# A hybrid decoder step on one core: the memory rows, the scan and the side chains at other places, with other paces and product banks

## The chip, the core and the metric

The kernel runs on one core of a Trainium2 chip. The core has a matrix engine (TensorE, PE in the profile, with a weight load PEld that overlaps it), a vector engine (VectorE, DVE), an activation engine (ScalarE, ACT), GpSimd (POOL) and a queue engine (SyncE, SP) that issues nearly all DMAs here. Each engine works through its own instructions in order and waits at the first one whose inputs or buffers are not there. The metric is the device time of one execution in microseconds, as the median of several runs.

## What is computed

One layer of a decoder in which three branches read the same normalized input. It is computed for 1024 prompt rows and for 8 x 4 sample rows, all in float32.

```python
def memory_kv(mem, mem_norm_g, w_mem_k, w_mem_v):        # 256 memory rows
    m = rmsnorm(mem, mem_norm_g)
    return m @ w_mem_k, m @ w_mem_v

def hybrid_layer(x, conv_state, ssm_state, mem_k, mem_v, ...):
    proj = rmsnorm(x, norm_g) @ w_in                     # 1024 -> 7696 columns
    gm_uv, gm_gate, ssm_z, ssm_xbc, ssm_dt, mem_q, mem_gate = split(proj)
    a_out = gmlp(gm_uv) * silu(gm_gate)                  # 128-row spatial mixing per head
    b_out = mamba2(ssm_z, ssm_xbc, ssm_dt, conv_state, ssm_state)   # conv, chunked scan, gated norm
    c_out = softmax_attention(mem_q, mem_k, mem_v) * silu(mem_gate)
    return x + concat(a_out, b_out, c_out) @ w_out       # 3072 -> 1024

y = rmsnorm(hybrid_layer(x), final_norm_g)               # prompt and sample rows
```

The scan of branch b goes over 8 chunks of 128 rows for each of 2 head groups, 16 chunk steps one behind the other. The sample rows bring their own state and their own memory keys and values (16 MB of them). States, convolution tails, memory keys and values and the gMLP's v rows are outputs too.

## The kernel before

**Precision.** A float32 product is made of three matmuls: each operand is split into a high part H (a copy rounded to fp32r, made on ACT) and a low part L (raw minus H, made on DVE or POOL), and `gemm3` (L330) issues H·H, H·L and L·H for each 128-row slice of the contraction. `split` (L120) makes H and L at once.

**Stages, in order of time.** (1) x rows are normalized, and z and dt columns are made row by row (0 to 125 us); (2) the gMLP's v columns, while the side makes sums of x blocks (to 222 us); (3) 22 *fast units*: each makes 256 output columns for all 1024 rows with seven products instead of eight (`unit`, L493), units 0 to 5 for the convolution, 6 to 9 for q, 10 and 11 for the first half of the memory gate, 12 to 15 for the gMLP gate, 16 to 19 for u, 20 and 21 for the rest of the memory gate (to 833 us); (4) four *plain units* of eight half products for the first third of the output projection, y_a (`unit_plain`, L543, to 988 us); (5) the memory's keys and values in 16 products of 128 rows x 256 columns, each 8 slices (to 1133 us); (6) the second third of the output projection beside the attention (to 1285 us); (7) the last third and the final norm, in 24 products of 128 columns x 384 or 288 rows (to the end). The outputs of a stage go to DRAM and come back when a later stage needs them.

**Product banks.** PSUM has three banks for unit and stage products (`mm_bank`, tags mm0 to mm2), four for everything else (`sd`) and one accumulator. In a fast unit product j writes bank (BANK[j] + 2u) mod 3. `mm()` takes the banks in turn and counts in `mmn`.

**Side chains.** All other work is written as Python generators, a *step* being the code between two `yield`s. After each slice of a product (three matmuls) `gemm3` calls `hook` (L323), which adds the current pace to a counter and, each time that the counter reaches one, puts the next step of the chain that stands first into every engine's program. A fast unit has 28 slices, a plain unit 32. So the pace (steps for each slice) and the yields fix what stands between which matmuls; nothing is decided at run time. A step's PE work stands in PE's own order and stalls the products when its input isn't there.

The chain beside units 6 to 15 (`side_chain`, L1683) does the sample convolution, `conv_out`, the samples' scan (`sample_scan`, state in and out at 0.26 steps a slice), the samples' scores and values (`sample_scores`, `sample_values`, also at 0.26, other steps at 0.8 to 1.0) and the gMLP tables (`gm_prep`). Beside unit 21 `a_load` fetches the a rows, which `a_split` splits into the operands of the plain units, over the buffers of the operands no longer read. Beside the plain units `scan_chain` (L1969) runs: the memory rows (`mem_prep`), the decay rows (`decay_rows`: POOL memsets, eight POOL DMAs into Rt, small row loads), and then `scan` (L1229) with five steps for each chunk, which goes on beside stage 5. `loadB` and `splitB` fetch the scan's results as the operand bH, bL of stage 6 when `SC_.done` says that they are stored.

**Late parts.** `u_split` (L445) puts the H part on ACT and notes the L part in `U.late`; `u_late` (L455) puts the noted L parts on DVE after the second slice of the next product, so that DVE does not wait for ACT ahead of the additions (L502) that free a product's bank.

**The tail.** Before the last stage five y tiles (`y_load`), the x rows of the first row block (`x_reload`) and the final gain (`gfin`) are fetched. Beside block b the c rows of block b + 1 are fetched (`c_load`) and split (`c_split`); `wo_get` splits the weights.

## Time and profile before

| what | us |
|---|---|
| median of 3 runs (lowest, highest) | 1412.37 (1410.91, 1418.32) |
| the profiled execution | 1416.92 |
| its span, first to last instruction | 1415.2 |
| PE busy in it | 1305.3 (92%) |
| DVE busy | 757.8 (54%) |
| ACT busy | 574.7 (41%) |
| POOL busy | 371.0 (26%) |
| mean granted PE clock | 0.958 of full speed |

All rows further down are from the profiled execution; their times are microseconds from its span's start. PE is busy nearly all the time, so a row in which PE is idle, or in which the granted clock is below 1, is time that the kernel loses; all other engines have slack on the average. A row of the timeline shows behind an instruction, in brackets, how long its engine stood idle before it and what ended that.

### The profile page before, as it was taken

Reading aid. Unit: us, or ns where it says so; the run is one execution under the profiler, and the core shown is the slowest. Engines: PE = TensorE matmul, PEld = TensorE weight load, DVE = VectorE, ACT = ScalarE, POOL = GpSimd, SP = SyncE. Lnnn points to the kernel's source line nnn. Section 1 sums busy time; section 2 is a strip of 40 time slices with the busy share of each in tenths; the row PEclk is TensorE's granted clock in tenths of the full one; section 3 lists DMA queues with packets and bytes.
Section 4 is the critical chain, followed back from the end, with each engine's and each line's share of the span. In section 5 each row is a group of like instructions: output and inputs, shape, how many; then the busy total and the mean of one; then the engine's idle time right before and its main releaser. Section 6 shows DMA issues by size and latency. Waiting matters only on the chain. (4 is left out here: it accounts for less than half of the span.)

```text
span 1415.2 us, 22019 instructions
## 1 busy us (share of the span) xinstructions
PE 1305.3 (92%) x8187; PEld 1098.8 (78%) x8187; DVE 757.8 (54%) x1260; ACT 574.7 (41%) x1163; POOL 371.0 (26%) x395
## 2 busy tenths in 40 slices
PE   8999998999889999999999987999777879997996
PEld 7999996787667777666788866767666779997986
DVE  6112536899544554433576653666677446643443
ACT  6222323554322243211477543455656334322232
POOL 4401623222435331221244303333322100000112
PEclk9999999999989999999999999999887899999998
DMA  7232221333345465374555543334555466656442
GB/s 232 71 100 80 81 84 37 103 101 107 98 122 165 139 206 176 117 227 122 160 174 165 209 132 101 118 90 149 177 161 161 141 197 216 194 162 212 147 146 95
DMA packets 215360, 200.76 MB, mean 142 GB/s; under 512 B 28445, under 2 KB 182129, under 8 KB 215253
## 3 DMA queue, kind: packets, MB, share of 16 engines
q1 hardware_dynamic: 214484, 198.95, 45.4%
q8 instruction: 65, 1.06, 0.3%
q0 software_dynamic: 768, 0.40, 0.2%
q14 instruction: 43, 0.34, 0.1%
HBM read 136.61 MB, written 62.43 MB: 141 GB/s over the span
## 5 line engine op out<-in xcount | busy, mean ns | idle before, releaser
L447 ACT ACTIVATE uh<-wst 128x512 fp32r<-128x512 f32 x88 | 55.3, 629 | 131.1 <-PE ps_mm L339 118.2
L455 DVE TENSOR_TENSOR ul<-wr,uh 128x512 fp32r<-128x512 f32 x82 | 70.8, 863 | 43.9 <-ACT uh L447 43.9
L127 DVE TENSOR_TENSOR wl<-wr,wh 128x512 fp32r<-128x512 f32 (+3 forms) x53 | 52.5, 1012 | 60.3 <-ACT wh L124 59.7
L447 ACT ACTIVATE uh<-wr 128x512 fp32r<-128x512 f32 x82 | 51.2, 625 | 77.8 <-PE ps_mm L339 74.8
L2272 POOL TENSOR_TENSOR xres<-xres,gfin 128x1536 f32<-128x1536 f32 (+3 forms) x6 | 14.3, 2385 | 250.7 <-ACT junk L2266 250.7
L455 DVE TENSOR_TENSOR ul<-wst,uh 128x512 fp32r<-128x512 f32 x88 | 66.0, 750 | 21.7 <-ACT uh L447 21.7
L338 PE MATMUL ps_mm<-bH,wh 128*128 128x384 f32 (+1 forms) x192 | 64.8, 337 | 6.8 <-ACT bH L124 5.8
L433 POOL TENSOR_TENSOR wst<-wr 128x512 f32<-128x512 f32 x22 | 28.9, 1314 | 135.1 <-DMA wr<-in_w_in_dram 81.6
L339 PE MATMUL ps_mm<-bL,wh 128*128 128x384 f32 (+1 forms) x192 | 63.1, 329 | 0.1
L340 PE MATMUL ps_mm<-bH,wl 128*128 128x384 f32 (+1 forms) x192 | 63.0, 328 | 0.0
L338 PE MATMUL ps_mm<-xB11H,uh 128*128 128x512 f32 x120 | 50.8, 423 | 7.2 <-DVE go L502 5.1
L996 DVE SCALAR_TENSOR_TENSOR ps_sd<-raw,vecs,ps_sd 128x512 f32<-128x512 f32 x72 | 54.2, 753 | 1.7
L124 ACT ACTIVATE wh<-wr 128x512 fp32r<-128x512 f32 (+3 forms) x60 | 46.9, 812 | 15.2 <-PE ps_mm L340 8.3
L338 PE MATMUL ps_mm<-xB22H,uh 128*128 128x512 f32 x120 | 49.7, 414 | 3.6 <-DVE go L502 3.6
L340 PE MATMUL ps_mm<-xB21H,ul 128*128 128x512 f32 x120 | 47.6, 396 | 2.3 <-DVE ul L455 2.3
L338 PE MATMUL ps_mm<-xB21H,uh 128*128 128x512 f32 x120 | 49.3, 411 | 0.0
L338 PE MATMUL ps_mm<-xT1H,uh 128*128 128x512 f32 x120 | 49.1, 409 | 0.0
L339 PE MATMUL ps_mm<-xB11L,uh 128*128 128x512 f32 x120 | 48.9, 407 | 0.0
L340 PE MATMUL ps_mm<-xB11H,ul 128*128 128x512 f32 x120 | 48.4, 403 | 0.0
L340 PE MATMUL ps_mm<-xB22H,ul 128*128 128x512 f32 x120 | 47.7, 397 | 0.0
L339 PE MATMUL ps_mm<-xB22L,uh 128*128 128x512 f32 x120 | 47.7, 397 | 0.0
L339 PE MATMUL ps_mm<-xB21L,uh 128*128 128x512 f32 x120 | 47.5, 395 | 0.0
(504 smaller groups left out, 4312.9 us busy)
## 6 DMA issues: line engine op xcount, KB each, us to landing
wr<-in_w_in_dram SPq DMA_DIRECT2D x56, 512.0 KB
wr<-in_w_out_dram SPq DMA_DIRECT2D x24, 512.0 KB
kv<-in_cache_mem_k_dram SPq DMA_DIRECT2D x16, 512.0 KB
kv<-in_cache_mem_v_dram SPq DMA_DIRECT2D x16, 512.0 KB
xt<-in_x_prompt_dram SPq DMA_DIRECT2D x8, 512.0 KB
z_d<-gt SPq DMA_DIRECT2D x32, 128.0 KB
v_d<-gt SPq DMA_DIRECT2D x32, 128.0 KB
xc_d<-cd SPq DMA_DIRECT2D x16, 256.0 KB
```

The lines of the kernel that those rows point to most:

```text
L124: ACT.activation(out=H, in_=raw, func=AF.Copy)
L127: leng.tensor_tensor(out=L, in0=raw, in1=rb(H), op=ALU.subtract)
L338: PE.matmul(out=ps, lhsT=lH, rhs=rH, start=(first and k == k0), stop=False)
L339: PE.matmul(out=ps, lhsT=lH, rhs=rL, start=False, stop=False)
L340: PE.matmul(out=ps, lhsT=lL, rhs=rH, start=False, stop=(last and k == k0 + kn - 1))
L433: POOL.tensor_tensor(out=t1, in0=A_(u, 2, 1), in1=A_(u, 2, 2), op=ALU.add)
L447: ACT.activation(out=h, in_=src, func=AF.Copy)
L455: DVE.tensor_tensor(out=l, in0=src, in1=rb(h), op=ALU.subtract)
L996: DVE.scalar_tensor_tensor(out=ps, in0=raw[:, 512 * h + j:512 * h + j + 512], scalar=cw(ct, j), in1=ps, op0=ALU.mult, op1=ALU.add)
L2272: eng.tensor_tensor(out=t[:, 0:nf, c0:c0 + w], in0=t[:, 0:nf, c0:c0 + w], in1=gc.unsqueeze(1).to_broadcast([128, nf, w]), op=ALU.mult)
```

## The change

No matmul is added or removed: PE has 6301 rows of program before and after. The instructions of the other engines are the same too, but for two DMAs that store the memory rows' H and L parts (1 MB each) and two that load them again. What changes is where things stand:

- **Banks.** Fast units use banks one further on; the plain units start at bank 0 (`mmn[0] = 2`).
- **Side steps.** `dt_chain` is cut into more steps (pace 0.25 for 0.3 in units 0 to 5). In units 6 to 15 quick steps go at 1.15 for 0.8 to 1.0, streams at 0.32 for 0.26, and `sample_scan` and `gm_prep` have more yields between steps that depend on each other. `conv_out` comes after the samples' values.
- **Memory rows.** `mem_prep` runs beside units 14 and 15, ahead of `gm_prep`, and stores its result in DRAM (`mem_d`); `mem_load` fetches it in the third plain unit.
- **Decay rows and scan.** `decay_rows` runs ahead of `a_load`, beside unit 20. `scan` begins with the first plain unit, at 0.47 steps a slice for 0.45, and goes on beside stage 5 at 0.28 for 0.37.
- **Splits of a.** Their L parts are made late; both parts of B22 follow product 6 of unit 21.
- **Tail.** Three c rows of block 1, the x rows of block 0 and the final gain are fetched within the attention's last steps; `c_load` runs further ahead and stands before `y_load`; x rows have a tile for each block.

```diff
-            ps = banks[j] = mm_bank((BANK[j] + 2 * u) % 3)
+            ps = banks[j] = mm_bank((BANK[j] + 2 * u + 1) % 3)
...
     def dt_chain(pool):
...
         DVE.scalar_tensor_tensor(out=ab, in0=xr, scalar=-1.0, in1=xr, op0=ALU.mult, op1=ALU.max)
+        yield
...
         ACT.activation(out=a_b, in_=a_b, func=AF.Exp)
+        yield
...
-    set_pace(0.3)
+    set_pace(0.25)
...
         split(psb[:32, 0:256], B3[0:32], B3[32:64], ACT, DVE)
+        yield
+        yield
...
+        for _ in range(2):
+            yield
         DVE.tensor_tensor(out=h3(xde), in0=h3(xdt), in1=hb(te_s, 32, NH), op=ALU.mult)
-        yield
-        yield
+        for _ in range(3):
+            yield
         split(xde, X3[0:32], X3[64:96], ACT, DVE)
+        for _ in range(3):
+            yield
...
-        set_pace(0.26)
+        set_pace(0.32)
...
-        set_pace(1.0)
+        set_pace(1.15)
...
+    mem_d = dpool.tile([2, 128, KD, 256], F32, name="mem_d")
+
+    def mem_prep(p):
+
+        g = p.tile([128, D], F32, name="mg_b")
+        SP.dma_start(out=g, in_=mem_norm_g.to_broadcast([128, D]))
+        HL = [p.tile([128, KD, 256], F32R, name="mem" + e) for e in "HL"]
...
+        for _ in range(5):
+            yield
...
+        for j in range(4):
+            rs[j // 2].s2(j % 2)
+            yield
+        for e in range(2):
+            SP.dma_start(out=mem_d[e], in_=rb(HL[e]))
+        yield
...
-            for _ in range(5):
+            for _ in range(7):
                 yield
...
-            yield
+            for _ in range(4):
+                yield
             ps = sd()
             PE.matmul(out=ps[:32, 0:256], lhsT=rep.rearrange("p b t -> p (b t)"), rhs=w4.rearrange("p h b t -> p (h b t)"),
...
-        with tc.tile_pool(name="cop", bufs=1) as p:
-            yield from conv_out(p)
         with tc.tile_pool(name="samp", bufs=1) as p:
             yield from sample_scan(p)
...
+        with tc.tile_pool(name="cop", bufs=1) as p:
+            yield from conv_out(p)
+        with tc.tile_pool(name="memp2", bufs=1) as p:
+            yield from mem_prep(p)
         yield from gm_prep()
...
-        set_pace(0.8)
+        set_pace(1.15)
...
+    def a_load():
+        yield from decay_rows()
...
-            split(AB.t[nm][:, ks, :], OA[nm][0][:, ks, :], OA[nm][1][:, ks, :], ACT, DVE)
+            src, H, L = AB.t[nm][:, ks, :], OA[nm][0][:, ks, :], OA[nm][1][:, ks, :]
+            ACT.activation(out=H, in_=src, func=AF.Copy)
+            U.late.append((L, src, H))
...
+    def a_last():
+        a_split("B22", 0)()
+        a_split("B22", 1)()
...
     def scan_chain():
-        yield from mem_prep()
-        m2_ctx.close()
-        yield from decay_rows()
         SC_.p = c_ctx.enter_context(tc.tile_pool(name="ssd", bufs=1))
...
-        set_pace(0.45)
-
+        set_pace(0.47)
+
+    def mem_load():
+        for e, t in enumerate((M.H, M.L)):
+            SP.dma_start(out=rb(t), in_=mem_d[e])
+
+    mmn[0] = 2
     for i in range(4):
-        spill(2 * i, y_d, AF.Copy, {0: scan_open} if i == 0 else None, X=OA, xs=AB.s)
+        spill(2 * i, y_d, AF.Copy, {0: {0: scan_open}, 2: {0: mem_load}}.get(i), X=OA, xs=AB.s)
...
-    set_pace(0.37)
+    set_pace(0.28)
...
             c_split(0, k, 2)
-            yield
+            if k < 6:
+                c_load(1, k // 2, 1)
+            yield
+        xres[0] = hp.tile([128, 3, D], F32, name="xres0")
+        x_rows(0)
+        gf.append(hp.tile([128, D], F32, name="gfin"))
+        SP.dma_start(out=gf[0], in_=final_norm_g.unsqueeze(0).to_broadcast([128, D]))
+        yield
...
         for ct in range(8):
+            if b < 2 and ct < 5:
+                c_load(b + 1, ct + 3, 1)
+            elif b < 1:
+                c_load(2, ct - 5, 1)
             y_load(8 * b + ct + 5)
-            if b < 2 and ct < 6:
-                if ct == 0:
-                    c_load(b + 1, 0, 1)
-                c_load(b + 1, ct + 1, 1 if ct < 5 else 2)
```

Three places show what this does to the order on an engine.

SP beside unit 15, before the change, where the gMLP tables are fetched (gg_d is the spilled gate, wr a weight tile, wsp the spatial weights that PE transposes first):

```order
L189 DMA gg_d<-go 128x512
L189 DMA gg_d<-sr 128x2x32
L214 DMA wr<-in_w_in_dram 128x4x256
L1613 DMA os_d<-os_s 128x8x32
L1635 DMA wsp<-in_gm_w_spatial_dram 128x8x128
L1636 DMA gnb_b<-in_gm_norm_b_dram 128x1024
L1637 DMA gng_b<-in_gm_norm_g_dram 32x1024
```

And after it:

```order
L189 DMA gg_d<-go 128x512
L189 DMA gg_d<-sr 128x2x32
L214 DMA wr<-in_w_in_dram 128x4x256
L1665 DMA mem_d<-memH 128x2048
L1665 DMA mem_d<-memL 128x2048
L1687 DMA wsp<-in_gm_w_spatial_dram 128x8x128
L1688 DMA gnb_b<-in_gm_norm_b_dram 128x1024
```

The two stores of the memory rows, 1 MB each, now stand directly ahead of wsp.

PE within the first plain unit (22), before, in the second half of its products (L316 are the transposes of the normalized memory rows):

```order
L338 MATMUL ps_mm<-xB11H,uh 128x512
L339 MATMUL ps_mm<-xB11L,uh 128x512
L340 MATMUL ps_mm<-xB11H,ul 128x512
L316 MATMUL ps_sd<-ident,xn 128x128 x4
L338 MATMUL ps_mm<-xB11H,uh 128x512
L339 MATMUL ps_mm<-xB11L,uh 128x512
L340 MATMUL ps_mm<-xB11H,ul 128x512
```

And after, in its fourth product (L1162, L1163, L1166 and L1200 are the first PE work of the scan's chunk 0, lines 1155, 1156, 1159 and 1193 of before):

```order
L338 MATMUL ps_mm<-xB22H,uh 128x512
L339 MATMUL ps_mm<-xB22L,uh 128x512
L340 MATMUL ps_mm<-xB22H,ul 128x512
L1162 MATMUL ps_sd<-bc 128x128
L1163 MATMUL ps_sd<-ident,bc 128x128
L1166 MATMUL ps_sd<-ident,xk 128x128 x4
L1200 MATMUL ps_sd<-Rt,Lt 128x512
L338 MATMUL ps_mm<-xB22H,uh 128x512
```

The memory rows' transposes are gone from the unit, and the scan's first matmul stands 25 slices (75 product matmuls) earlier than before, where it came in unit 23.

SP from the end of the attention into the tail, before (gt and y_d belong to stage 6, cr are c rows, ys y tiles, xres x rows):

```order
L1910 DMA y_d<-gt 128x288
L1898 DMA gt<-y_d 128x384
L214 DMA wr<-in_w_out_dram 128x8x128
L1910 DMA y_d<-gt 128x384
L1898 DMA gt<-y_d 128x288
L1910 DMA y_d<-gt 128x384
L1910 DMA y_d<-gt 128x288
L2199 DMA ys<-y_d 128x384 x5
L2206 DMA xres<-in_x_prompt_dram 128x1024 x3
L2213 DMA gfin<-in_final_norm_g_dram 128x1024
L2199 DMA ys<-y_d 128x384
L2173 DMA cr<-c_d 128x384 x2
```

And after:

```order
L2225 DMA cr<-c_d 128x384 x3
L1973 DMA y_d<-gt 128x288
L1961 DMA gt<-y_d 128x384
L2217 DMA xres_12572<-in_x_prompt_dram 128x1024 x3
L2209 DMA gfin<-in_final_norm_g_dram 128x1024
L214 DMA wr<-in_w_out_dram 128x8x128
L1973 DMA y_d<-gt 128x384
L1961 DMA gt<-y_d 128x288
L1973 DMA y_d<-gt 128x384
L1973 DMA y_d<-gt 128x288
L2250 DMA ys<-y_d 128x384 x5
L2225 DMA cr<-c_d 128x384
```

The first c rows, the x rows and the gain have moved from behind the five ys loads to ahead of the last gt loads.

## Rows read from the trace of the kernel before

**Rows 1.** The page's first part, PE: busy us (share), instructions.

```profile
PE 1305.3 (92%) x8187; PEld 1098.8 (78%) x8187; DVE 757.8 (54%) x1260; ACT 574.7 (41%) x1163; POOL 371.0 (26%) x395
```

**Rows 2.** Busy time by stretch: window and length, then engines, granted PE clock, DMA share, GB/s.

```profile
222.00:245.00 23.00, 19.22 (x86) 14.13 (x87) 13.87 (x35) 9.73 (x19) 5.86 (x8) 0.85 0.10 31
366.00:510.00 144.00, 133.83 (x686) 98.80 (x685) 72.90 (x108) 44.27 (x82) 66.21 (x59) 0.92 0.46 135
510.00:660.00 150.00, 150.00 (x870) 101.56 (x868) 58.83 (x94) 40.58 (x70) 25.11 (x20) 1.00 0.54 175
660.00:700.00 40.00, 36.00 (x164) 27.67 (x163) 18.17 (x29) 10.34 (x16) 8.21 (x9) 0.91 0.53 150
820.00:840.00 20.00, 13.79 (x53) 10.66 (x52) 10.94 (x14) 8.83 (x12) 0.00 (x0) 0.91 0.44 150
840.00:890.00 50.00, 42.74 (x239) 32.81 (x239) 17.02 (x30) 19.10 (x35) 16.29 (x29) 0.93 0.40 115
890.00:988.00 98.00, 91.26 (x606) 68.11 (x605) 61.92 (x106) 51.95 (x120) 35.20 (x42) 1.00 0.36 109
988.00:1133.00 145.00, 112.98 (x854) 97.49 (x852) 94.35 (x152) 82.55 (x191) 36.33 (x45) 0.85 0.55 162
1133.00:1160.00 27.00, 19.32 (x106) 18.48 (x107) 11.67 (x20) 8.93 (x16) 0.00 (x0) 0.87 0.84 245
1290.00:1381.00 91.00, 76.91 (x440) 74.47 (x439) 36.72 (x59) 23.73 (x55) 12.28 (x6) 0.94 0.50 160
```

**Rows 3.** PE's waits, longest in total: total us, times, longest us.

```profile
PE ps_mm L338 <- DVE go L502: 9.8, 3, 5.1
...
PE ps_sd L1155 <- DMA bc<-bc_d: 6.5, 1, 6.5
PE ps_mm L338 <- ACT woH L124: 6.3, 1, 6.3
PE ps_mm L338 <- ACT bH L124: 5.8, 1, 5.8
PE ps_sd L1047 <- POOL csT L1027: 5.1, 1, 5.1
```

**Rows 4.** Timeline of PE in unit 6: start, us, instruction, before and behind the L1047 wait.

```profile
374.00 0.39 PE L339 MATMUL ps_mm<-xT4L,uh 128*128 128x512 f32 x1
...
374.68 0.39 PE L339 MATMUL ps_mm<-xT4L,uh 128*128 128x512 f32 x1
...
382.12 0.63 PE L340 MATMUL ps_mm<-xT4H,ul 128*128 128x512 f32 x1
382.55 0.63 PE L338 MATMUL ps_mm<-xB11H,uh 128*128 128x512 f32 x1
```

**Rows 5.** Timeline of PE, the waits at the start of unit 0.

```profile
222.48 0.50 PE L338 MATMUL ps_mm<-xB11H,uh 128*128 128x512 f32 x1 [2.01 <-DVE gt L384]
...
234.91 0.50 PE L340 MATMUL ps_mm<-xB21H,ul 128*128 128x512 f32 x1 [2.26 <-DVE ul L455]
```

**Rows 6.** Timeline of POOL, first and last instruction of the samples' convolution (nine in all).

```profile
370.90 1.35 POOL L1019 TENSOR_TENSOR cvs<-rs,vecs 128x384 f32<-128x384 f32 x1
...
379.89 0.47 POOL L1027 COPY csT<-rs 128x288 f32<-128x288 f32 x1
```

**Rows 7.** Timelines of SP and of PE, the spatial weights' load and its first reader.

```profile
665.45 0.37 SPq L1635 DMA_DIRECT2D wsp<-in_gm_w_spatial_dram  x1
...
669.54 1.09 PE L1649 MATMUL ps_sd<-ident,wsp 128*128 128x128 f32 x4 [2.34 <-DMA wsp<-in_gm_w_spatial_dram]
```

**Rows 8.** SP's own waits, the one of the scan's first load.

```profile
SPq L1115 <- DMA Rt<-Rraw: 8.6, 4, 6.7
```

**Rows 9.** Timelines of SP and ACT at the tail's start.

```profile
1292.75 1.38 SPq L2206 DMA_DIRECT2D xres<-in_x_prompt_dram  x3
...
1296.10 1.28 SPq L2173 DMA_DIRECT2D cr<-c_d  x2
...
1304.11 0.52 ACT L124 ACTIVATE cH<-cr 128x384 fp32r<-128x384 f32 x1 [18.39 <-DMA cr<-c_d]
```

131 lines of the change are left out of this document (68 added, 63 removed).

## Prediction

> **What bounds the kernel now.** The page comes first: PE is busy for 1305.3 of 1415.2 us and every other engine for at most 54% [rows 1]. The change neither adds nor removes a matmul, so its time can only come from what PE loses. PE loses in two ways: it stands idle, or it runs at the lower granted clock. The second view is the table by stretch [rows 2]: length less PE busy is the idle time, and length times (1 - granted clock) is about what the lower of the two levels (1.2 for 2.4 GHz) cost there. Six stretches in ten carry it, and one by far the most:
>
> - 222 to 245 (start of unit 0): 3.8 idle + 3.5 clock = 7.2
> - 366 to 510 (side chain's start, samples' scan): 10.2 + 11.5 = 21.7
> - 510 to 660 (sample streams): 0
> - 660 to 700 (gMLP tables): 4.0 + 3.6 = 7.6
> - 820 to 840 (last fast unit to first plain one): 6.2 + 1.8 = 8.0
> - 840 to 890 (scan's start): 7.3 + 3.5 = 10.8
> - 890 to 988 (plain units beside the scan): 6.7 + 0 = 6.7
> - 988 to 1133 (keys and values beside the scan): 32.0 + 21.8 = 53.8
> - 1133 to 1160 (stage 6 begins): 7.7 + 3.5 = 11.2
> - 1290 to 1381 (tail): 14.1 + 5.5 = 19.6
>
> Together 146.6 us, the most that the change could touch. Third come the waits and their timelines [rows 3 to 9], which say what each loss is. What the clock does is seen in the product matmuls: 0.23 us apart before PE's wait for L1047, and 0.43 apart after it [rows 4]. So a wait of several microseconds is paid nearly twice, and one that goes takes its slow stretch along.
>
> One slice of a unit is three matmuls, so 0.69 us [rows 4]; a keys-and-values slice has half the columns, which I estimate at 0.35.
>
> **The change part by part.** Gains are counted against the profiled execution (1416.9, span 1415.2).
>
> *Banks and dt_chain, 7.2 now.* Unit 0 waits 2.0 us because its bank is the one that the last v product still holds, then 2.3 because DVE, stuck behind dt_chain's chain of ACT results, makes ul late [rows 5]. With the bank one further on, unit 0 finds one that was freed two products earlier; dt_chain's steps stand four slices apart, 2.8 us, against instructions below 1 us. I take a gain of 5 (3 to 7).
>
> *Side chain's start, 21.7 now.* PE waits 5.1 for the samples' convolution [rows 3], which takes POOL 370.9 to 380.4 [rows 6]. Its first PE reader now comes 12 slices behind the chain's start, 8.3 us and two sample matmul groups, against 9.5: a wait of 0 to 1. The next loss is an addition (L502) that stands on DVE behind a split waiting for ACT, one of three such waits of 9.8 together [rows 3]; now two to three yields lie between such steps. The slow stretch behind both should go in part, but sixteen 8-column matmuls for the decay stay where they are and may hold the clock down. Gain 14.5 (6 to 20).
>
> *Streams at 0.32 for 0.26, 0 now.* A 512 KB load every 3.1 slices for 3.8. The stretch moves 175 GB/s at a DMA share of 0.54 [rows 2]; 1.2 times that is 0.65. Below zero there is nothing to gain, since PE is never idle there. Cost 1 (0 to 6).
>
> *Memory rows beside units 14 and 15, 7.6 now.* Their PE work is moved, not added, and hides where the products are. New are the waits. From the loads to the first transposes lie 11 slices, 7.6 us, and a sample group: about right for 1.5 MB at the tail's rate (below), a square on ACT and a product on DVE, so 0 to 3 of wait. Then two 1 MB stores go out on SP directly ahead of wsp. From the last memory transposes to wsp's first reader lie 27 matmuls, 6.2 us. SP can issue the stores only after the last split, by my estimate 2 us later, and wsp 1.4 after that; wsp needs 4.1 from issue to use when nothing large is ahead [rows 7]: ready at 7.7, a wait of 1.5. If the 2 MB go first, at the 280 GB/s of the tail (2.6 MB between 1292.8 and 1304.1, less an estimated 2 for the latency, [rows 9]), it is 7 us more: a wait of 7 to 8. The tail's c rows, which landed only 8 us after their issue with 2 MB ahead of them [rows 9], are nearest to that case. I take 5.5, and 5 for the clock behind it and 1.5 for the first transposes: 12, a loss of 5 (12 lost to 5 gained). SP's stores of the gate stand behind it, and nobody waits for them. The Trainium skill, "DMA: Bandwidth & Descriptors" (Queues, rings and completion order), says that each DMA engine takes its descriptors in ring order, which speaks against this part: by that, the wait is the 7 to 8 us and the whole sum 2 us worse; by wsp's own row alone it is 1.5 and the sum 4 us better.
>
> *Late splits of a, bank 0 first, 8.0 now.* The two L502 waits here are 6.2 idle: DVE makes a large L part of a ahead of the addition that frees a bank, and the first plain unit starts in the bank of the last product. Both go. The decay rows now keep POOL beside unit 20, longer than the 6.7 us that SP waits for them now [rows 8], in front of the sums for unit 21; those have about 8 slices (5.5 us) of slack, so 0 to 2 lost. Gain 6 (3 to 8).
>
> *Scan's start, 10.8 now.* PE waits 6.5 for the first bc tile [rows 3]. The cause is on SP: it holds the scan's first load (L1115) for 6.7 us until the Rt DMAs have read a buffer that it lies over [rows 8]. With the decay rows 50 slices earlier that wait is gone; next late is the load itself, issued 8 slices (5.5 us) and a sample group ahead. Gain 7 (3 to 10).
>
> *Scan beside plain units and keys and values, 60.5 now.* The program gives 5 steps to a chunk. Before, 8.8 chunk loops fall into the keys and values, 13.5 slices each; after, 5.9, with 17.9 slices each. In the plain units 10 instead of 7, at 10.6 slices for 11.1. So a step is covered by 0.93 us of products in the keys and values now, 1.53 in the plain units, and the losses for a loop are 6.1 and 1.0. After, the cover is 1.23 and 1.47: on the line between the two rows, 3.6 and 1.5. DVE would then be busy about 80% of a loop (94.4 us in 145 now, a third less time for each loop's work at most [rows 2]), so I take 4.5 rather than 3.6. That makes 5.9 x 4.5 + 10 x 1.5 = 41.6: a gain of 18 (0, if the keys and values keep 6.1 and the plain units rise to 2.5; 38, if they come down to 2). The 2 MB reload in the third plain unit delays an xk load by up to 7 us, with a loop of 14 us ahead: nothing.
>
> *Stage 6 begins, 11.2 now.* PE waits 5.8 for the last split of bH [rows 3], because the scan's last store comes 8 slices before the end. Now it comes 18 before, 3.5 us earlier. Gain 7 (2 to 10).
>
> *Tail, 19.6 now.* ACT stands idle for 18.4 us until the first c rows land, with the x rows and gain ahead of them [rows 9], and the weights' split behind it costs PE 6.3 [rows 3]. That goes, and with it most of what follows in the stretch. But the 2 MB now stand ahead of the last gt loads and the ys loads, whose sums stand on DVE ahead of a weight split: up to 7 us of new wait, of which I take 5, plus 4 for the clock. Gain 9 (0 to 17).
>
> Sum: 5 + 14.5 - 1 - 5 + 6 + 7 + 18 + 7 + 9 = 60.5, so 1416.9 becomes 1356. The profiled execution lies 4.5 above the median of the three runs, 1412.4; the same gain from that gives **1352**.
>
> **The rivals.** *Half of it.* The scan's chain, not its cover, sets the loop (gain 6), the stores are ahead of wsp in full (12 lost) and the tail only trades waits (2 gained): 38.5 of the others + 6 - 12 + 2 = 34.5, 1378. For it: DVE at 80%, one xk buffer, four sd banks. Against it: the same loop ran at 14 us with hardly a wait in the plain units.
>
> *More.* The keys and values come down to the plain units' level, wsp comes in time for what it costs now, the tail is smooth: 38.5 + 36 + 0 + 15 = 89.5, 1323.
>
> *Slower.* One mechanism could do it: the scan begun with the output projection meets in all its 16 loops what it meets in the keys and values now (waits for sd banks that DVE and ACT free late), and more. The other terms give 42.5, so the scan's loss would have to grow from 60.5 to 103, 6.4 for each loop, against 6.1 now at the worst place. At 8 it is 1437. For it: plain units too must split weights on DVE. Against it: 1.0 for each loop there now.
>
> *The scan does not really start earlier,* since its first loads are held again, by the buffers of a: 7 and some 4 of the scan's gain are lost, 1363, within the forecast's reach.
>
> **How the numbers follow.** Forecast, 1336 to 1367: 0.57 (with the last rival). Half: 0.24. More: 0.12. Within 0.5% (7 us, about what a measurement of this kernel can tell from no change): 0.03. Slower: 0.04. The likeliest is 1352. The range runs to both neighbours, 1324 to 1386: it leaves out about half of "more" and the ends of "half", and the slower cases. Faster by over 0.5%: 0.93, the first three; same 0.03; slower 0.04.
>
> **What would show it.** Right, if PE's wait list has lost L1047, bc, woH and bH and the L502 waits; if the keys and values take about 100 us instead of 145, at a clock above 0.9; if a new wait of some 5 us stands at wsp, and a smaller one at the tail's first weight split. Wrong, if the chunk loop stays at 16.5 us there (145 / 8.8) whatever the pace, or if PE waits in the sample streams or for the memory rows.

## The result, and the profile after

The changed kernel takes **1392.38 us** (median of 4 runs, 1390.72 to 1397.39), against 1411.71 for the kernel before beside it: a ratio of 0.9859, 95% interval 0.982 to 0.9898. Forecast were 1352, 1324 to 1386. The direction was right; of a gain of 60.5 us, 19.3 came (26.2 between the two spans, 1415.2 and 1389.0). PE is still the only engine near its limit; the page's first part, as [rows 1]:

```profile
PE 1294.5 (93%) x8187; PEld 1092.4 (79%) x8187; DVE 766.2 (55%) x1262; ACT 575.4 (41%) x1166; POOL 373.6 (27%) x395
```

The table by stretch, with the columns of [rows 2], in stretches of after that hold the same work:

```profile
221.00:244.00 23.00, 22.93 (x111) 17.66 (x110) 18.30 (x34) 12.19 (x20) 7.12 (x12) 1.00 0.20 59
360.00:510.00 150.00, 144.17 (x788) 106.57 (x790) 81.24 (x119) 50.00 (x91) 71.28 (x61) 0.97 0.54 164
510.00:640.00 130.00, 128.09 (x748) 85.71 (x744) 48.22 (x79) 31.87 (x56) 19.96 (x15) 1.00 0.50 161
640.00:700.00 60.00, 49.11 (x213) 37.27 (x204) 28.70 (x40) 18.07 (x30) 13.58 (x15) 0.80 0.51 161
805.00:832.00 27.00, 22.43 (x108) 16.83 (x108) 16.53 (x21) 12.39 (x21) 3.62 (x3) 1.00 0.83 278
832.00:870.00 38.00, 31.69 (x176) 24.41 (x174) 19.24 (x31) 17.34 (x32) 7.76 (x9) 0.96 0.39 121
870.00:1000.00 130.00, 119.57 (x805) 89.51 (x806) 80.29 (x140) 71.32 (x164) 45.25 (x54) 0.98 0.42 127
1000.00:1114.00 114.00, 90.46 (x697) 80.26 (x696) 77.48 (x121) 67.20 (x151) 22.77 (x28) 0.84 0.62 181
1118.00:1142.00 24.00, 19.31 (x113) 19.03 (x112) 7.58 (x14) 5.66 (x10) 0.00 (x0) 0.86 0.85 242
1272.00:1365.00 93.00, 85.27 (x518) 83.77 (x517) 43.13 (x77) 25.54 (x63) 14.00 (x8) 0.94 0.48 151
```

With the prediction's measure (length less PE busy, plus length times one less the clock) each term of its sum has its answer:

| term | lost before | lost after | gain | forecast |
|---|---|---|---|---|
| banks, dt_chain | 7.2 | 0.1, and 1.2 at 252.9 | 5.9 | 5 (3 to 7) |
| side chain's start | 21.7 | 10.3 | 11.4 | 14.5 (6 to 20) |
| streams | 0 | 1.9 | -1.9 | -1 (-6 to 0) |
| memory rows, tables | 7.6 | 22.9 | **-15.3** | -5 (-12 to 5) |
| late splits of a | 8.0 | 4.6 | 3.4 | 6 (3 to 8) |
| scan's start | 10.8 | 7.8 | 3.0 | 7 (3 to 10) |
| scan beside plain units, keys and values | 60.5 | 13.0 + 41.8 | **5.7** | 18 (0 to 38) |
| stage 6 begins | 11.2 | 8.1 | 3.1 | 7 (2 to 10) |
| tail | 19.6 | 13.3 | 6.3 | 9 (0 to 17) |
| sum | 146.6 | 125.0 | 21.6 | 60.5 |

The sum lacks 4.6 us of the spans' difference. Over the whole spans the same measure gives 169.3 us lost before and 145.9 after, 23.4 apart, so some 2 us were won outside these stretches; the 3 that remain it does not see, and no run shows what they are. Of the missing 39 us, the scan's loop has 12, the memory rows 10, and five other places 2.6 to 4 each. PE's list of waits (total us, times, longest), as [rows 3] for before, has new names where most of the old ones stood.

```profile
PE ps_sd L1189 <- DVE BL L127: 7.5, 6, 2.8
PE ps_mm L338 <- DVE gt L1972: 6.5, 2, 4.7
PE ps_sd L1701 <- issue: 6.1, 1, 6.1
PE ps_mm L340 <- DVE wl L127: 5.5, 1, 5.5
PE ps_sd L316 <- issue: 4.8, 1, 4.8
...
PE ps_sd L1162 <- DMA bc<-bc_d: 4.7, 1, 4.7
...
PE ps_mm L340 <- DVE ul L455: 3.8, 1, 3.8
...
PE ps_mm L338 <- DVE go L502: 2.7, 2, 1.5
```

L1701 reads the spatial weights wsp, L316 the memory rows' norm, L1162 opens a chunk of the scan, L1189 is its state product. L1047, woH and bH have left the list, as the prediction asked; bc has not, and the L502 waits have shrunk from 9.8 us to 2.7.

### The profile page after: what moved, and what is told of

It reads as the page before. It is cut to its first block, busy times and chain, and to the rows that moved or that the text cites. A ratio compares the mean times of both kernels' runs of the same rounds, so it can differ in the third digit from the quotient of the medians.

```text
span 1389.0 us, 22033 instructions
## 1 busy us (share of the span) xinstructions
PE 1294.5 (93%) x8187; PEld 1092.4 (79%) x8187; DVE 766.2 (55%) x1262; ACT 575.4 (41%) x1166; POOL 373.6 (27%) x395
## 4 chain that ended last, share of the span: by engine, by line
PE 74%; DVE 6%; DMA 6%; issue 5%; ACT 4%; POOL 2%; SPq 1%; POOLq 0%; ACTq 0%; DVEq 0%
PE ps_mm L338 19%; PE ps_mm L340 18%; PE ps_mm L339 18%; PE ps_sd L1264 1%; PE ps_acc L1617 1%; PE ps_acc L1555 1%; PE ps_sd L1818 1%; PE ps_acc L488 1%; PE ps_sd L1570 1%; PE ps_sd L316 1%; ACT wh L124 1%; DMA gt<-y_d 1%; DMA aB<-a_d 1%; PE ps_sd L488 1%; DVE wl L127 1%
## 5 line engine op out<-in xcount | busy, mean ns | idle before, releaser
L340 PE MATMUL ps_mm<-xT1H,ul 128*128 128x512 f32 x120 | 47.5, 396 | 3.8 <-DVE ul L455 3.8
L339 PE MATMUL ps_mm<-xT1L,uh 128*128 128x512 f32 x120 | 47.4, 395 | 0.0
```

Source lines behind the costliest of these rows:

```text
L339: PE.matmul(out=ps, lhsT=lH, rhs=rL, start=False, stop=False)
L340: PE.matmul(out=ps, lhsT=lL, rhs=rH, start=False, stop=(last and k == k0 + kn - 1))
```

## Experiments

All are edits of the kernel after, and their times stand beside its 1392.4 and its ratio of 0.9859 to the kernel before.

### The scan's loop: both sides alone

```diff
-    set_pace(0.28)
+    set_pace(0.0)
     for blk in range(8):
```

> Change to the kernel after: the scan stands still through the keys and values (pace 0) and its last 5 to 6 loops run behind them with no products beside them. It measures both by themselves. Theory (the loop is a chain through ACT, DVE and POOL that is longer than PE's own 6 us): a loop alone takes 11 us or more, so that even a loop with 12 us of PE's work in the keys and values has no slack where the chain's parts fall together, and the keys and values alone take 50 to 60 us (128 slices, 45 us, and some waits for weights). Rival (a loop alone takes 8 us or less, and the keys and values alone 70 us or more, as their own splits and loads set their time): then the keys and values are the limit and not the scan. In all slower than after: 1400 to 1425.

Measured: 1410.2 (one run). The two stretches, keys and values alone and then four loops of the scan alone (columns as above):

```profile
1003.00:1061.00 58.00, 53.16 (x400) 52.26 (x399) 30.19 (x45) 30.36 (x59) 0.00 (x0) 0.90 0.85 248
1071.00:1118.00 47.00, 28.12 (x196) 19.79 (x196) 32.04 (x54) 23.95 (x58) 16.26 (x19) 0.72 0.24 70
```

A loop alone takes **11.7 us** (11.2 to 12.2, from one state product to the next), with PE busy for 60% of it at a granted clock of 0.72; the keys and values alone take 58 (first to last of their products). Both are what the theory asked for. The first and the last state product, four loops apart:

```profile
1071.55 0.80 PE L1189 MATMUL ps_sd<-xdH,BH 128*128 128x512 f32 x1 [2.44 <-ACT sz L1112]
...
1118.23 0.79 PE L1189 MATMUL ps_sd<-xdH,BH 128*128 128x512 f32 x1 [4.76 <-ACT xdH L124]
```

Together they took 113 in after, with 5.9 loops, and 140 before, with 8.8: (113 - 58) / 5.9 = 9.3 for a loop, and (140 - 58) / 8.8 = 9.3 as well, if the 58 of this one run hold for before too. So a loop costs about the same there at either pace (e6 below, with some 6.5 loops, gives 10.5), and saves no more than 2.4 of its 11.7 us. By the prediction's measure the keys and values alone already lose 4.8 idle and 5.8 to the clock, 10.6 in all, while they move 248 GB/s (181 in after). As far as this stays when the scan stands beside them, it belongs to no loop, and the loops lose (53.8 - 10.6) / 8.8 = 4.9 us each before and (41.8 - 10.6) / 5.9 = 5.3 after; the prediction divided the whole loss by the loops. Beside the plain units a loop takes 14.2 with 10.6 slices of 0.69 in it, so it costs 6.9. A loop moved from the one place to the other is worth 2.4 us, and 2.9 were moved: 7, against the 5.7 measured.

### The scan's loop: pace

```diff
-        set_pace(0.47)          # plain units
+        set_pace(0.60)          # e6: 0.45
...
-    set_pace(0.28)              # keys and values
+    set_pace(0.20)              # e6: 0.37
```

> Change to the kernel after: the scan's pace only, 0.60 steps a slice beside the plain units instead of 0.47, and 0.20 in the keys and values instead of 0.28, so that some 12.5 loops fall into the plain units (8.3 slices each) and 3.6 into the keys and values (25 slices each). Theory (products beside a step decide, as in the prediction's line from 1.0 lost at 1.53 us a step to 6.1 at 0.93): a step has 1.15 us of products in the plain units and 1.75 in the keys and values, so the plain units lose about 4 a loop and the keys and values less than 1: in all some 50 us as in after's 55, the keys and values' loops nearly free of loss. Rival (the splits that keys and values and scan share on ACT and DVE decide there, whatever the pace): the loss for a loop stays at 6 to 8 us in the keys and values, the plain units stay below 2 a loop, and the whole comes to 13 x 1.5 + 3.6 x 7 = 45, 1380 to 1386.

> Change to the kernel after: the scan's pace as in the kernel before, 0.45 and 0.37, with the rest of after kept, so that a loop in the keys and values has 13.5 slices as before and the scan ends some 30 slices earlier. Theory (products beside a step decide): the loss for a loop there rises against after's, as after's was to fall against before's; the stage becomes longer, 1394 to 1402. Rival (the shared splits decide): a loop loses 5.5 to 7 us as in both kernels, the stage has as many loops as in after or half a loop more, and the time is within 4 us of after, 1388 to 1396.

Measured: 1406.5 (ratio 0.9925, 0.9897 to 0.9952) and 1391.6 (0.9829, 0.9776 to 0.9883). Loops from one state product to the next, in the keys and values:

| kernel | slices a loop | mean loop there | stage | loop in plain units | median |
|---|---|---|---|---|---|
| before | 13.5 | 16.1 | 139.9 | 14.6 | 1411.7 |
| e6, pace as before | 13.5 | 16.1 | 126.5 | 14.5 | 1391.6 |
| after | 17.9 | 18.4 | 113.1 | 14.2 | 1392.4 |
| e5, 0.60 and 0.20 | 25 | 17.7 (one) | 88.9 | 13.9 | 1406.5 |
| e7, bL on POOL | 17.9 | 17.4 | 110.4 | 14.3 | 1388.8 |
| e16, bH and bL on POOL | 17.9 | 16.9 | 110.7 | 14.6 | 1390.5 |
| e1, rows earlier | 17.9 | 18.4 | 115.4 | 14.5 | 1394.1 |
| e9, keys' own bank | 17.9 | 19.0 | 112.0 | 14.1 | 1390.4 |
| e12, split earlier | 17.9 | 17.0 | 108.1 | 13.9 | 1383.8 |
| e10, both | 17.9 | 17.4 | 105.4 | 13.8 | 1380.8 |

(The table counts from state product to state product, the expectations from chunk to chunk.) A third more products beside each step make the loop longer, not its loss smaller; the pace of after won nothing over that of before. At 0.60 a loop beside the plain units costs 8.2 instead of 6.9. And e5 shows a second cost, which both theories missed: once the scan has ended, ACT stands for the scan's rows (yb), with the weights' split behind them, and PE behind that. ACT, then PE, of e5:

```profile
1103.55 0.63 ACT L124 ACTIVATE bH<-yb 128x512 fp32r<-128x512 f32 x1 [6.47 <-DMA yb<-yb_d]
...
1105.90 2.11 ACT L124 ACTIVATE wh<-wr 128x512 fp32r<-128x512 f32 x3
```

```profile
1106.60 0.58 PE L338 MATMUL ps_mm<-wh,memH 128*128 128x256 f32 x1 [4.24 <-ACT wh L124]
```

### The scan's loop: amount of work

```diff
-            split(t[:, :, :tsz(c)], bH[:, ks, ts_], bL[:, ks, ts_], ACT, DVE)
+            split(t[:, :, :tsz(c)], bH[:, ks, ts_], bL[:, ks, ts_], POOL, POOL)   # e7: ACT, POOL
```

> Change to the kernel after: the L parts of the scan's rows (bL, 18 subtractions of 0.65 us) are made on POOL, not on DVE. Theory (shared splits on ACT and DVE decide in the keys and values): DVE there is busy for 77 of 114 us and waits for ACT nearly all of the rest, so 11.5 us less of its work shortens the stage by 5 to 11 us: 1381 to 1388. Rival (too few products beside a step): no change but for POOL's slower instructions, 1390 to 1395. A third (POOL, at about 1.3 us for each, becomes late with xdL and MT and holds up DVE by its own accesses): slower, 1395 to 1405.

> Change to the kernel after: both parts of the scan's rows (bH and bL, 36 instructions, about 10 us of ACT and 11 of DVE) are made on POOL, which is busy for 23 of 114 us there; the keys and values then share that much less of ACT and DVE with the scan. Theory (the amount of work that the two share sets the loop): the loops beside the keys and values fall from 20.1, 18.2 and 19.4 to 16 or less, and the stage by 10 us or more: 1376 to 1384, but for what POOL's last parts cost at the start of stage 6. Rival (the order in each queue sets it, as the earlier split showed): loops of 17.5 us or more, 1386 to 1394, or slower where POOL's xdL now stands behind these parts.

Measured: 1388.8 (0.9821, 0.9776 to 0.9865) and 1390.5 (0.9833, 0.9808 to 0.9858). In e16 the stage has 57.8 and 69.8 us of ACT and DVE where after has 67.2 and 77.5, and PE loses as much:

```profile
1002.00:1112.00 110.00, 86.38 (x688) 77.43 (x686) 69.81 (x102) 57.81 (x133) 56.85 (x61) 0.83 0.61 181
```

The loops became 1 to 1.5 us shorter, half of what the theory asked or less, and the medians are 2 to 4 us lower, which their intervals do not tell from none. That the amount of work is a part of it is read from the loops of these traces, and no more. POOL's help was not free either: the weights' splits of 128x512 on DVE took 1058 ns on the average in e16, against 747 in after.

### The scan's loop: order and banks

ACT of after in one loop there: it waits 2.8 us for DVE's gate product, and the next chunk's weighted rows (xdH), the finished rows (sz, which free a bank of sd) and BH stand behind that wait; then PE, which waits for the bank.

```profile
1031.46 0.63 ACT L1097 ACTIVATE sz<-xsD 128x512 f32<-128x512 f32 x1 [2.84 <-DVE xsD L1095]
...
1032.09 0.61 ACT L124 ACTIVATE xdH<-xde 128x512 fp32r<-128x512 f32 x1
1032.61 1.12 ACT L1112 ACTIVATE sz<-ps_sd,vecs 128x128 f32<-128x128 f32 x4
1033.61 0.29 ACT L124 ACTIVATE BH<-ps_sd 128x128 fp32r<-128x128 f32 x1
```

```profile
1033.79 0.69 PE L2051 MATMUL ps_sd<-ident,kst 128*128 128x128 f32 x2 [2.46 <-ACT sz L1112]
```

```diff
 # e1: the finished rows ahead of the norm, into a buffer of their own
+                    yo = SC_.p.tile([128, 512], F32, tag="t1", name="yo", bufs=1)
+                    fy = y_T2(r, 128, gp_, cp_ * 128, yo)
...
 # e9: the keys' transposes
-        ps = sd()
+        ps = acc_bank()
...
 # e12: two steps earlier; e10: e9 and e12
-            if nx:
-                sXsplit(i + 1)
             fs = []
...
+            if nx:
+                sXsplit(i + 1)
             pd = sd()
```

> Change to the kernel after: the scan's scaled output rows of the chunk before (four ACT instructions, y_T2) go into a buffer of their own and are issued before the gate norm of this chunk, no longer behind its square. Theory (crossed queues): in the keys and values ACT stands 2.8 us in every loop for DVE's gate product, and the rows, which free the sd bank that PE asks for next, stand behind it; PE's waits for these rows (13.3 us of idle, and the slow clock behind them) go, the loop falls from about 18.5 to 16.5 us, and the run comes out 8 to 16 us below the kernel after, at 1376 to 1384. Rival (too few products beside each step): the wait only changes its name, 1389 to 1395. Rival (DVE's amount of work): DVE has nothing less to do, 1389 to 1395.

> Change to the kernel after: the transposes of the keys (k_T, one bank of sd for each key product, up to eight of them while the scan runs) use the bank that the units' samples used, which is free here, and no longer one of the four sd banks that the scan takes in turn. Theory (bank ring): with one k_T between, the scan's decay product meets the bank of the rows just transposed (PE waits for ACT's sz L1112) and its state product the bank whose B part DVE is still making (PE waits for DVE's BL); in the plain units, where the scan has the four banks alone, the same loop loses about 1. The waits L1200 and L2051 for ACT's sz (8.5 us) and L1189 for DVE's BL (7.5) go while keys are made, the loops there fall from 20.1, 18.2 and 19.4 to some 16, and the run comes out 6 to 14 us lower, 1378 to 1386. Rival (chain through ACT and DVE, as the two runs before showed that a wait only changes its name): the loops keep 18 us or more, 1389 to 1395.

> As the run with the keys' own bank, and the split of the next chunk's weighted rows (xdH on ACT, xdL on POOL) stands two steps earlier in the loop, ahead of the gate norm for which ACT waits 2.8 us, instead of behind it. Theory (crossed queues, second part): the state product's waits for xdH and xdL (4.6 us and about 1 us in most loops, plain units too) go as well, 4 to 10 us below the run with the bank alone, 1370 to 1380. Rival (the norm's chain itself is what is late): no more than 2 us below that run.

> Change to the kernel after: only the earlier split of the next chunk's weighted rows (xdH, xdL two steps earlier, ahead of the gate norm); the keys' transposes keep their sd bank. Theory (the split behind the norm is the cause, the bank is not): as the run with both, 1379 to 1384, loops of some 16 us in the keys and values. Rival (both are needed, each hides the other): 1387 to 1393, loops of 18 us, PE waiting for ACT's sz (L1112) and DVE's BL as in after.

Measured: e1 1394.1 (0.9838, 0.9803 to 0.9873), e9 1390.4 (0.9837, 0.9808 to 0.9865), e10 **1380.8** (0.9761, 0.9739 to 0.9783), e12 **1383.8** (0.9746, 0.970 to 0.9793). e1's theory fell: PE's waits for sz went, and waits for BL of up to 5.2 us came, where 2.8 had been the longest. e9's fell too, its loops grew. e12's theory held in the time (1379 to 1384), while its loops came to 17.0, not 16. The split alone does nearly all, in the plain units as well (13.8 to 13.9 a loop); whether the bank adds to it is not settled (3 us by the medians, nothing by the ratios). The stretches of e10, plain units and keys and values, against 870 to 1114 above:

```profile
866.00:998.00 132.00, 121.95 (x833) 93.31 (x832) 90.74 (x146) 73.81 (x168) 48.54 (x57) 0.99 0.43 130
998.00:1103.00 105.00, 83.58 (x691) 75.10 (x690) 77.86 (x120) 67.07 (x151) 24.21 (x28) 0.92 0.67 194
```

So 11.4 + 29.8 = 41 are lost there, against 55 in after. The 30 that are left in the keys and values (10.6 of them lost there even without the scan, e17) were not taken away by any run; e15 below, which put more of DVE's order right, changed nothing.

### Memory rows and the spatial weights

In after, SP issues wsp's load 6 us behind the second store of the memory rows, and POOL, whose fills go into the same place, says what for (SP, POOL, PE):

```profile
652.86 0.33 SPq L1665 DMA_DIRECT2D mem_d<-memH  x1
653.58 0.33 SPq L1665 DMA_DIRECT2D mem_d<-memL  x1
659.51 0.38 SPq L1687 DMA_DIRECT2D wsp<-in_gm_w_spatial_dram  x1
```

```profile
659.57 0.20 POOL L1692 MEMSET one_r<- 1x128 f32 x1 [11.13 <-DMA mem_d<-memL]
```

```profile
646.18 1.09 PE L316 MATMUL ps_sd<-ident,xn 128*128 128x128 f32 x4 [4.79 <-issue]
...
663.78 1.08 PE L1701 MATMUL ps_sd<-ident,wsp 128*128 128x128 f32 x4 [6.10 <-issue]
```

```diff
+        with tc.tile_pool(name="wspp", bufs=1, side="right") as wp_:
+            wsp = wp_.tile([128, 8, 128], F32, name="wsp")
             with tc.tile_pool(name="memp2", bufs=1) as p:
                 yield from mem_prep(p)
+            yield from gm_prep(wsp)
```

> Change to the kernel after: the spatial weights wsp get 4 KB of their own, so that their load does not write where the memory rows' parts lie; the stores of the memory rows still stand ahead of it on SP. Theory (buffer): in the trace of after wsp's load was not issued until both stores had landed (issue at 659.5, stores at 652.9 and 653.6), so it will now be issued within 1 us of them and PE's wait of 6.1 us at the first wsp transposes becomes 0 to 2.5, with some slow clock gone: 1382 to 1388. Rival (queue order, as the prediction had it): the load is issued early but its data come only behind the 2 MB of stores; the wait stays 5 us or more, 1390 to 1395.

Measured: 1391.1 (0.9822, 0.9752 to 0.9891). The load was issued at once, and was not early (SP, PE of e2):

```profile
654.12 1.24 SPq L1686 DMA_DIRECT2D wsp<-in_gm_w_spatial_dram  x1
```

```profile
662.40 1.09 PE L1700 MATMUL ps_sd<-ident,wsp 128*128 128x128 f32 x4 [4.58 <-DMA wsp<-in_gm_w_spatial_dram]
```

8.3 us from issue to use, against 4.1 in [rows 7] with nothing ahead, and 4.3 in after, where the buffer had held the load until the stores were done. The theory was wrong and the rival nearly right (a wait of 4.6 where it asked for 5 or more): the stores cost the wait by either road, and the buffer only 1.5 us on top. The Trainium skill, "DMA: Bandwidth & Descriptors" (Queues, rings and completion order), has each engine take its descriptors in ring order; e2 agrees, with 8.3 us behind 2 MB.

Then the rows' own wait was given time (e8, part b), and last the order was changed (e14, below):

```diff
 # (a) conv_samples
+        for _ in range(9):
+            yield
         ACT.activation(out=cvs, in_=cvs, func=AF.Silu)
...
 # (b) mem_prep
-        for _ in range(5):
+        for _ in range(12):
             yield
...
 # (c) attention
-        x_rows(0)
+        for j in range(3):
+            SP.dma_start(out=xres[0][:, j], in_=xp_rows[j * 128:(j + 1) * 128, :])
+            yield
+            yield
```

> Three changes to the kernel after, in stretches that lie far apart and are read one by one in the trace. (a) Side chain's start: nine more steps before ACT's silu of the samples' convolution, and DVE's first instruction that needs POOL's fills two steps later. Theory (ACT and DVE stand for POOL, and the weights' parts behind them are what PE misses): PE's 3.8 us for ul goes, with 3 us of slow clock. Rival (the chain is only as late as before at its next reader): PE waits 3 us or more at the next place. (b) Memory rows: seven more steps between their loads and the norm, one more before and two more behind each product of the norm, two fewer at the end. Theory (10.8 us from load to first transposes against 6 of cover): the 4.8 us wait falls below 1; wsp's wait of 6.1 stays at 5 to 7. (c) The tail: the x rows of the first block are loaded one at a time, two steps apart, and the gain after them. Theory (the last gt load lands 7.6 us after its issue, behind 2 MB): the waits of 1.8 and 5.5 fall to 2 or less together, as does the slow stretch behind them. Rival: the last gt load is still behind a row of x or the gain and 4 us or more stay. All three by theory: some 20 us, 1370 to 1376; by the rivals 1386 to 1392.

Measured: 1383.8 (0.9794, 0.9739 to 0.9849), between its theory and its rivals; by its parts:

(a) The wait for ul went, and one of 3.5 us came at 393 (for an addition that stands on DVE behind the split of the samples' rows); the low clock of that stretch was gone in e8, and two thirds back in e11. That ACT and DVE had stood for POOL is plain in after's rows (ACT, DVE, PE):

```profile
373.15 0.52 ACT L1033 ACTIVATE cvs<-cvs 128x384 f32<-128x384 f32 x1 [5.87 <-POOL cvs L1031]
```

```profile
375.56 0.25 DVE L1342 TENSOR_SCALAR Ls<-accTs 16x32 f32<-16x32 f32 x1 [7.81 <-POOL Cm L1357]
```

```profile
376.46 0.51 PE L340 MATMUL ps_mm<-xT1H,ul 128*128 128x512 f32 x1 [3.78 <-DVE ul L455]
```

(b) The rows' wait of 4.8 went to 0, but wsp's grew from 6.1 to 7.9: the side chain has no slices left there. Unit 15 ends, the rest is drained, and wsp's eight transposes stand in a row with no product between them.

(c) The wait of 1.8 went; of the 5.5, 5.0 stayed. Behind the last gt load stood a second cause, in SP and DVE of e8: the first ys loads are issued only when the last product of stage 6 has read the operand that their buffers lie over, and the weights' split stands on DVE behind their sum.

```profile
1270.09 2.23 SPq L2254 DMA_DIRECT2D ys<-y_d  x5
```

```profile
1272.66 0.55 DVE L2370 TENSOR_TENSOR ys<-ys,ps_mm 128x384 f32<-128x384 f32 x1 [6.87 <-DMA ys<-y_d]
1273.14 1.22 DVE L127 TENSOR_TENSOR wl<-wr,wh 128x1024 fp32r<-128x1024 f32 x1
```

### The scan's start, and stage 6

```diff
 # e3, in scan()
+            if i == 0:
+                for _ in range(3):
+                    yield
             if nx:
                 sA(i + 1)
```

> Change to the kernel after: three more steps between the scan's first chunk and its second (nothing else). Theory (the wait moved to the second chunk): the wait of 4.7 us at the scan's start is that of the second chunk's rows, which can only be loaded when the first chunk's have left their one buffer, 5.5 us ahead of their use; with three steps (6.4 slices, 4.4 us) more, it falls under 1 us and takes about 2 us of slow clock along, while the scan ends three steps later in the keys and values (about 2 us): 1386 to 1390. Rival (the transfers themselves are late whenever they are asked for, as 280 GB/s are moved there): 3 us or more of the wait stay, 1391 to 1397.

Measured: 1386.5 (0.978, 0.9742 to 0.9818). The wait for bc is gone and the stretch runs at full clock, as the theory had it. It had been the wait for the second chunk's load: in after SP issued it at 845.75, when the first chunk had left the one buffer, PE was there 1.4 us later, and the load took 6.1:

```profile
851.87 0.77 PE L1162 MATMUL ps_sd<-bc 128*128 128x128 f32 x2 [4.74 <-DMA bc<-bc_d]
```

In return the scan ends later, and the wait at stage 6's start is again one for bH, 6.7 us.

```diff
 # e4
         y_open(0)
+        y_open(1)
+        vr_load()               # was ahead of outproj
```

> Change to the kernel after: at the start of stage 6 the first two loads of partial sums (gt) are issued ahead of the reload of the memory values (vr), not behind it. Theory (next in the queue): the 4.7 us that PE waits for DVE's first sum there come from SP, which holds the vr load for 4.7 us until its data have been stored, with the gt loads behind; the wait goes, and the slow stretch of 7 us behind it: 1384 to 1388. Rival (the values' parts, vL, become the next late thing, or the gt loads wait for their buffers): PE waits as long somewhere in the next 15 us, 1390 to 1394.

Measured: 1391.6 (0.9816, 0.9777 to 0.9856). In after SP spends 4.65 us on vr, whose rows must first be stored, and gt's loads stand behind (SP, DVE):

```profile
1120.96 4.65 SPq L2092 DMA_DIRECT2D vr<-mv_d  x2
1125.66 0.90 SPq L1961 DMA_DIRECT2D gt<-y_d  x2
```

```profile
1129.56 0.55 DVE L1972 TENSOR_TENSOR gt<-gt,ps_mm 128x384 f32<-128x384 f32 x1 [7.68 <-DMA gt<-y_d]
```

The rival was right: 1.7 of the 4.7 stayed, and 3.4 came at the first attention product, which reads the queries, loaded behind vr.

### The sums

e11: e8, e3 and e4, ys in a buffer that lies free, and 13 steps more ahead of wsp's reader. e13: e10, e3 (pace 0.50), e4, e8 (c) and ys. e14: e13 and e8 (a), the streams at 0.36, and

```diff
-        with tc.tile_pool(name="memp2", bufs=1) as p:
-            yield from mem_prep(p)
         yield from gm_prep()
+        with tc.tile_pool(name="memp2", bufs=1) as p:
+            yield from mem_prep(p)      # row by row, ten steps from load to norm
```

e15: e14, e1 and DVE's hL ahead of the sums.

> All the changes to after that touch other places than the scan's loop, together: side chain's start, memory rows and the tail's x rows as in their run; thirteen steps more between the spatial weights' load and their first reader (wsp landed 8.3 us after its issue when the 2 MB of stores were ahead of it and no buffer held it, and was held 5.5 us more by the buffer); the tail's first partial sums (ys) in a buffer that does not lie over the operand of the product before (their load was issued only when that product had ended); the scan's second chunk three steps later; the first gt loads ahead of vr. Theory: each place loses what its wait was: wsp 7.9 to under 1.5, the tail's 5.0 to under 2, the scan's start 4.7 to under 1, stage 6 to 4 or so (the operand's last split is next, since the scan ends later), side start 3.5 stays; with the clock behind them some 30 us less than after, 1358 to 1368. Rival (each wait has another a microsecond behind it, as at the samples' start): half of it, 1372 to 1380.

> The mended places together, with the memory rows and the side chain's start as in after: keys' own bank, earlier split of the weighted rows, three steps before the scan's second chunk with its pace at 0.50 for 0.47, gt ahead of vr, x rows of the tail one at a time, ys in a buffer of its own. Theory (the terms stand side by side): from after's 1392.4 less 11.5 (scan's loop), 6 (scan's start), 6.5 (tail) and 0 to 2 (stage 6), 1366 to 1370. Rival (what is won beside the keys and values is waited for in stage 6): 1372 to 1380.

> As the run before, and in the side chain: the gMLP tables are made first and the memory rows after them, row by row, with ten steps from the loads to the norm; nine more steps before ACT's silu at the chain's start; the three streams at 0.36 for 0.32, which makes room for both. Theory (the memory rows cost after 13 us more than the tables alone had cost before, as they were given neither time nor a place behind the tables): the loss of 20 us in that stretch falls to 7 (as before, 7.6) and the samples' start by some 4: 1349 to 1356. Rival (the loss follows the memory rows: their stores now hold the next loads, gg and v, and the units behind wait; or the streams cannot go at 0.36): 10 us or more stay, 1360 to 1368.

> As the run before, and in the scan's loop the scaled rows of the chunk before go ahead of the norm into a buffer of their own (as in the first run of this study), and DVE's low part of the state (hL) ahead of the two additions before the norm. Theory (DVE's order is what is left: PE waits there for BL and hL by 1.8 to 3.2 us a loop): 3 to 8 us below the run before. Rival (the loop's chain is as long as before, the wait only changes its name, as the first run showed): within 2 us of it.

Measured: e11 1378.5 (0.9745, 0.972 to 0.9769), e13 1377.6 (0.9708, 0.9662 to 0.9754), e14 **1366.1** (0.9619, 0.9565 to 0.9673), e15 1367.4 (0.9637, 0.9588 to 0.9686). e11, e13 and e14 ended 8 to 11 us above the upper end of what their theories gave, within the ranges of their rivals. Places that lie apart are not independent: e11's wsp waited 9.0, because the steps added ahead of it were drained; e13's keys and values took some 4 us longer than e10's (109 against 105), and stage 6 still waits 5.0 us, for SP stands there for weights' buffers that ACT frees behind the scan's last rows. e15 is no better than e14. e14 settles the memory rows: with the tables first, wsp waits 0.2 and the rows 2.3. Its three stretches (side chain's end, scan's start, tail):

```profile
615.00:690.00 75.00, 72.56 (x347) 55.69 (x346) 37.42 (x57) 24.11 (x41) 15.08 (x16) 0.91 0.54 167
823.00:855.00 32.00, 30.78 (x182) 24.44 (x182) 17.80 (x29) 16.74 (x31) 6.43 (x6) 1.00 0.43 124
1245.00:1340.00 95.00, 90.84 (x561) 89.70 (x560) 43.78 (x77) 26.79 (x64) 14.02 (x8) 0.98 0.54 174
```

That is 9.2 lost at the tables and rows together, against 22.9 in after; 1.2 at the scan's start, against 7.8; 6.1 in the tail, against 13.3. At 1366.1, e14 beats both kernels, and lies 14 above the forecast (6 by its ratio).

## Why the prediction failed, by its steps

- **Banks and dt_chain**: right, 5.9 for 5; unit 0's two waits of 2 us are gone, and dt_chain's own of 1.0 is now one of 1.2, at 252.9.
- **Scan beside the keys and values**: the step that failed is the line through the two rows, loss a loop against products beside a step. The two rows differ in more than their products: in the keys and values ACT and DVE have the weights' and rows' splits in the same queues. By it a loop should lose 3.6 there, taken as 4.5 for DVE's sake; it lost 41.8 / 5.9 = 7.1, where it had been 6.1. The stage took 113 us at a clock of 0.84 instead of about 100 above 0.9. What the runs put in its place: a chain of 11.7 us through PE, ACT, DVE and POOL (e17), of which the keys and values hide no more than 2.4, most likely because their own work on ACT and DVE is added to it in the same queues. That work is 37 us on each engine in after (wh 18.7, bH 9.8, kst 5.7, kH 3.1 on ACT), 5.2 for 17.9 slices; 11.7 and 5.2 are 16.9, near the 18.4 measured (for the 13.5 slices of before, 11.7 and 3.9 are 15.6, for 16.1). This sum is an estimate, from a chain measured at a clock of 0.72. Shown is that more products beside a step (after, e5) do not shorten the loop or the run, and that the order (e12) does; that the amount of work does (e16) is only indicated. The prediction had this as its first rival (the chain, not its cover, sets the loop), and gave it the lesser chance; its 1378 was too low as well, as the 38.5 that it kept for the other six terms came to 24.9. What sets the 30 us that e10 still loses there is open, but for the 10.6 that e17 has without the scan.
- **Memory rows**: three sizes. wsp's wait, 6.1 for 5.5, came out near by luck, as the buffer that held the load was not thought of (with a buffer of its own, e2, 4.6 are left); the rows' first wait was 4.8 for 1.5, as the chain from load to transposes (10.8 us: 6 of transfer, square, norm, product) was held against 7.6 by eye and not added up, and PE was there after 6.0; and the low clock took 12 for 5, over three stretches, the last of them from 671 to 682, with PE busy throughout. (Two sums of this part are loose: 1.5 and 7 are 8.5, not 7 to 8, and 12 less 7.6 is 4.4, not 5. Neither changes the account.)
- **Scan's start**: right that the held load goes; the question what is late next was put for the first chunk's load alone. The second chunk's, one buffer deep, was late: 4.7 of the 6.5 us came back.
- **Stage 6**: bH's wait went as forecast, and gt behind vr, not named, took its place (4.7 of 5.8).
- **Tail**: the new wait was named and sized (7.4 for 5); the ys loads stood behind it as a second cause.
- **Side chain's start**: PE's own reader was given 8.3 us, and was in time; ACT's and DVE's instructions that also wait for POOL were not looked at, and what PE missed stood behind them.
- **Late splits of a**: 3.4 for 6; three waits of 1.2 to 1.8 stayed in unit 21. **Streams**: 1.9 for 1.

All nine terms have the right sign, and eight of nine came out worse than forecast, mostly since the wait that goes was priced in full and the next one behind it at little or nothing; the scan's line and the memory rows' chain are reasons of their own. The range let the terms miss independently; most of them missed together, for that one reason.

## To carry to other kernels

A wait that is removed is worth the distance to the next thing that is late in the same place, so write down for PE, ACT, DVE and SP what each would wait for next before the gain is counted. Work moved beside other work was hidden here only in small part where the two meet in the same in-order queues: run each side alone once (here 11.7 us a loop and 58 us), and compare their sum with the two together. The load that was asked for behind large stores was late with or without a buffer of its own (e2); what helped was to change the order (e14).

## What the runs showed of the hardware

The granted clock fell to its lower level in e14 although PE had been idle for no more than 0.2 us in the 60 us before: it did the tables' plain 128-column products, between the weights' products. Two neighbouring windows:

```profile
630.00:636.00 6.00, 6.00 (x34) 4.59 (x31) 4.29 (x7) 0.63 (x1) 0.00 (x0) 1.00 0.83 246
636.00:644.00 8.00, 8.00 (x23) 5.72 (x23) 3.40 (x5) 0.00 (x0) 0.00 (x0) 0.51 0.16 49
```

So the low clock at the tables goes only in part with the wait. And an instruction on DVE took nearly twice its time while POOL worked on tensors; POOL and DVE of after, the same operation of DVE with POOL busy (643.7 to 647.2) and idle:

```profile
643.71 1.28 POOL L437 TENSOR_TENSOR wst<-wr 128x512 f32<-128x512 f32 x1
```

```profile
643.79 2.29 DVE L308 SCALAR_TENSOR_TENSOR xn<-mem,rstd,mg_b 128x1024 f32<-128x1024 f32 x1 [8.30 <-POOL rstd L287]
...
648.47 1.28 DVE L308 SCALAR_TENSOR_TENSOR xn<-mem,rstd,mg_b 128x1024 f32<-128x1024 f32 x1 [0.72 <-POOL rstd L287]
```

The Trainium skill, "SBUF — State Buffer" (SBUF: two separate sides), has DVE, when it reads two tensors, and GpSimd take one pair of ports in turn, each for a whole instruction. The rows agree: DVE took 1.0 us more, and POOL's instruction still had 1.2 us to go when DVE's began. The norm's product was priced nowhere in the prediction with POOL beside it.
